# A transformer and state-space block on one core: three product groups with 512 moving columns are issued as halves of 256

## The chip, the cores and the metric

The kernel runs on one core of one Trainium2 chip. The metric is the device time of one execution in microseconds (us); three executions of the kernel before took 1441.66, 1443.39 and 1445.95 us, median 1443.39 us. The rows come from one profiled execution, with one clock for all engines of the core.

## The reference, cut to what matters

Two blocks are computed on 256 tokens of width 1024, all in fp32. The first ends in a layer of experts, the second in a feed-forward layer. Three sums of many products are what the change touches:

```python
# experts: 16384 experts, each with a row of u and a row of v; wgt is zero for those not chosen
wgt = gc * gelu(u . x)
out = einsum('chk,chkd->cd', wgt, vv)          # the kernel: W[256 x 16384] @ v[16384 x 1024]
# second block
h  = layer_norm(ALPHA * h + mix @ w_o)         # [256 x 1024] @ [1024 x 1024]
ff = square(relu(h @ w_up + b_up)) @ w_down    # the last: [256 x 4096] @ [4096 x 1024]
```

The kernel does not gather expert rows: it computes all 16384 activations, multiplies them by a gate matrix that is zero where an expert was not chosen, and multiplies the result by the whole of v.

## The kernel before, in words

**Products in three parts.** An fp32 matrix is split into a high part hi, rounded to the type fp32r, and a rest lo = x - hi. A product of x and w is then three matmuls, hi·hi, hi·lo and lo·hi, all accumulated in one place of PSUM. That is `mm3` (L219 to L225): L221 takes the high weights and the high moving operand, L224 the high weights and the low moving operand, L225 the low weights and the high moving operand. TensorE loads the weights anew ahead of every one of these matmuls. The first matmul of a sum carries `start=True`.

**The split.** `split_tile` (L193) takes a loaded tile `raw` of 128 x 1024, makes `hi` on ScalarE (L198) and `lo` on VectorE (L201). `raw`, `hi` and `lo` have three buffers each, so the split of a later tile waits until TensorE has finished with the tile three before. The loads are issued on SyncE's queue in a written order (L188).

**The order of the stages in the experts.** `expert_in` (L996) runs 128 times over tiles of u: the tile is the weights, the 256 tokens are the moving operand, and the output `ea` has 256 columns; 24 matmuls each. While it runs, `gates` (L1013) puts in groups of eight small fp16 matmuls of 128 columns (`gt`, L1034 and L1035). Then `sum_rows` (L1069) runs over 128 tiles of v ("terms"): `expert_out` (L1050) splits the 128 x 256 weights of that term into `whi` (L1056) and `wlo` (L1057), and the tile of v is now the moving operand. `rows_of` (L1060) goes over two halves h of the 1024 output columns for one group t of 128 tokens. The four sums `acc[t][h]` of 128 x 512 fp32 fill one PSUM bank each, named `pe` in the rows. One term is 2 x 2 x 3 = 12 matmuls with 512 moving columns.

**The last terms.** `sum_rows` holds back the last three terms and then goes bank by bank through `HALVES`: the three terms of bank (0,0), then of (0,1), (1,0), (1,1), each bank's first matmul ordered after the last of the bank before (`before`), so that VectorE can read a finished bank while TensorE fills the next.

**The same function twice more.** `w_o` (L1233) is `sum_rows` over 8 terms, `ff` (L1268) over 32 terms; in the latter each term is preceded by the 24 matmuls `up` (L1252, 256 moving columns) of a later feature tile, whose output becomes the weights of its own term. In all `rows_of` issues (128 + 8 + 32) x 12 = 2016 matmuls.

**Who orders the work.** The order of instructions on each engine is made when the program is built, by a scheduler that goes by the written order, by what is ready in its own simulated time, and by the written ordering edges (`after`). In `pe` it puts the four L221 of a term first and then four pairs of L224 and L225; in `ff` it keeps the written order L221, L224, L225. The other products of the second block, `pj` (L1424, 256 or 272 moving columns), have the moving operand hT, whose eight slices are 288 columns apart.

Of the kernel before, what the change touches and what calls it, by code (L numbers as in the profile page):

```python
# [81 lines left out]
class K:  # L82
# [977 lines left out]
    def rows_of(self, acc, t, x, v, first, last, before=None, halves=(0, 1)):  # L1060
        x = [z[:, t * 128:t * 128 + 128] for z in x]
        for h in halves:
            done = self.mm3(
                acc[t][h], x, [z[:, h * 512:h * 512 + 512] for z in v], first, last, before
            )
        self.last = done
        return done

# [788 lines left out]
```

## Time and profile before

| what | value |
|---|---|
| median of three executions | 1443.39 us |
| the profiled execution, its own time | 1441.46 us |
| its span, first to last instruction | 1439.7 us |
| TensorE busy | 1376.3 us, 96% |
| VectorE busy | 1126.6 us, 78% |
| ScalarE busy | 763.2 us, 53% |
| granted TensorE clock, mean | 0.985 |
| stage `ea` (first to last start) | 203.0 to 593.8 us |
| stage `pe` | 593.8 to 955.4 us |
| stage `w_o` | 1219.0 to 1242.2 us |
| stage `up` and `ff` | 1251.1 to 1427.7 us |

Matmuls overlap in TensorE's pipeline, so the duration of one is longer than the distance to the next; the distance from start to start is the pace at which TensorE works. "PEld" is the weight load of TensorE, which runs beside the matmul before it.

### The profile page before, as it was taken

The page shows a single profiled execution, that of the slowest core. Times are in us where ns is not written, and L with a number is a line of the kernel's source. Part 1 is how long each engine was busy: PE and PEld are TensorE (multiplying, and loading weights), DVE is VectorE, ACT ScalarE, POOL GpSimd, SP SyncE. Part 2 cuts the span into 40 slices and gives each one's busy share as a digit, 9 for nine tenths or more (in the row PEclk, how much of TensorE's full clock was granted, in tenths as well). Part 3 has the DMA queues.
Part 4 walks back from the last instruction along what each step waited for, and adds up shares of the span by engine and source line. Part 5 has one row for each costly group of instructions (what it writes and reads, how often), then busy time and mean ns, then how long its engine had stood idle before and what let it go on. Part 6 is the DMA issues. An engine that isn't in the chain of part 4 may idle for free.

```text
span 1439.7 us, 24324 instructions
## 1 busy us (share of the span) xinstructions
PE 1376.3 (96%) x9217; PEld 1216.1 (84%) x9217; DVE 1126.6 (78%) x2329; ACT 763.2 (53%) x1324; POOL 150.2 (10%) x128
## 2 busy tenths in 40 slices
PE   6897999999999999999999999998999999999996
PEld 3686999999999999988887788877876899889995
DVE  6888899977889897655566798668798978665556
ACT  3365555545555544544446468645474564455552
POOL 0133000000000000000000000014656600000001
PEclk9998999999999999999999999999999999999998
DMA  9774445554444445555557765534232455366552
GB/s 384 291 268 146 176 148 192 189 192 170 161 168 162 170 162 170 192 190 189 189 191 275 256 213 191 190 136 147 88 129 78 147 179 198 111 204 199 189 191 93
DMA packets 72287, 263.20 MB, mean 183 GB/s; under 512 B 8149, under 2 KB 8533, under 8 KB 71786
## 3 DMA queue, kind: packets, MB, share of 16 engines
q1 hardware_dynamic: 72170, 261.66, 52.5%
q8 instruction: 72, 1.18, 0.3%
q14 instruction: 45, 0.37, 0.1%
HBM read 259.53 MB, written 2.10 MB: 182 GB/s over the span
## 4 chain that ended last, share of the span: by engine, by line
PE 75%; DVE 15%; ACT 4%; DMA 2%; issue 2%; POOL 1%; DVEq 0%; ACTq 0%; POOLq 0%
PE pe L224 8%; PE pe L221 8%; PE pe L225 8%; PE ea L225 7%; PE ea L224 7%; PE ea L221 7%; DVE lo L201 4%; PE ff L224 2%; PE ff L221 2%; PE ff L225 2%; PE up L224 2%; PE up L225 2%; PE up L221 2%; PE pj L221 1%; PE pj L224 1%
## 5 line engine op out<-in xcount | busy, mean ns | idle before, releaser
L201 DVE TENSOR_TENSOR lo<-raw,hi 128x1024 fp32r<-128x1024 f32 x398 | 489.6, 1231 | 173.0 <-ACT hi L198 170.4
L198 ACT ACTIVATE hi<-raw 128x1024 fp32r<-128x1024 f32 x398 | 419.8, 1055 | 382.1 <-issue 87.9
L225 PE MATMUL ea<-h,lo 128*128 128x256 f32 x1024 | 285.6, 280 | 1.7 <-DVE lo L201 1.5
L221 PE MATMUL ea<-h,hi 128*128 128x256 f32 x1024 | 285.1, 279 | 0.8 <-ACT s_lo L1006 0.8
L224 PE MATMUL ea<-h,hi 128*128 128x256 f32 x1024 | 285.6, 279 | 0.0
L224 PE MATMUL pe<-lo,whi 128*128 128x512 f32 x512 | 200.1, 393 | 0.8 <-DVE lo L201 0.8
L225 PE MATMUL pe<-hi,wlo 128*128 128x512 f32 x512 | 198.7, 393 | 0.0
L225 PEld LDWEIGHTS ea<-h,lo 128*128 128x128 f32 x1024 | 192.1, 188 | 2.7 <-DVE lo L201 2.7
L221 PEld LDWEIGHTS ea<-h,hi 128*128 128x128 f32 x1024 | 192.5, 188 | 1.0 <-ACT s_lo L1006 1.0
L224 PEld LDWEIGHTS ea<-h,hi 128*128 128x128 f32 x1024 | 192.5, 188 | 0.0
L221 PE MATMUL pe<-hi,whi 128*128 128x512 f32 x512 | 143.5, 395 | 1.1 <-ACT hi L198 1.1
L224 PEld LDWEIGHTS pe<-lo,whi 128*128 128x128 f32 x512 | 96.1, 188 | 24.1 <-DVE lo L201 1.9
L221 PEld LDWEIGHTS pe<-hi,whi 128*128 128x128 f32 x512 | 95.6, 188 | 23.3 <-ACT hi L198 1.7
L225 PEld LDWEIGHTS pe<-hi,wlo 128*128 128x128 f32 x512 | 96.1, 188 | 21.9
L221 PE MATMUL pj<-hT,hi 128*128 128x256 f32 (+1 forms) x328 | 96.6, 294 | 0.0
L224 PE MATMUL pj<-hT,hi 128*128 128x256 f32 (+1 forms) x328 | 93.9, 286 | 2.5 <-DVE hT L217 2.5
L225 PE MATMUL pj<-hT,lo 128*128 128x256 f32 (+1 forms) x328 | 93.5, 286 | 0.0
L1056 ACT ACTIVATE whi<-s_lo 128x256 fp32r<-128x256 f32 x64 | 26.3, 417 | 78.2 <-PE pe L224 78.2
L221 PEld LDWEIGHTS pj<-hT,hi 128*128 128x128 f32 x328 | 62.8, 191 | 5.7 <-issue 2.7
L225 PE MATMUL up<-h1T,lo 128*128 128x256 f32 x240 | 66.9, 279 | 0.4 <-DVE lo L201 0.4
L221 PE MATMUL up<-h1T,hi 128*128 128x256 f32 x240 | 66.8, 279 | 0.2 <-ACT hi L198 0.2
L224 PE MATMUL up<-h1T,hi 128*128 128x256 f32 x240 | 67.0, 279 | 0.1
(471 smaller groups left out, 2745.4 us busy)
## 6 DMA issues: line engine op xcount, KB each, us to landing
raw<-in_u SPq DMA_DIRECT2D x128, 512.0 KB, 3.5
raw<-in_v SPq DMA_DIRECT2D x128, 512.0 KB, 4.2
raw<-in_sC SPq DMA_DIRECT2D x41, 512.0 KB, 3.5
raw<-in_down SPq DMA_DIRECT2D x32, 512.0 KB, 4.2
raw<-in_up SPq DMA_DIRECT2D x30, 512.0 KB, 4.2
s_hi<-in_ada SPq DMA_DIRECT2D x28, 512.0 KB, 6.0
raw<-in_sA SPq DMA_DIRECT2D x17, 512.0 KB, 4.3
s_hi<-in_sA SPq DMA_DIRECT2D x14, 512.0 KB, 6.2
```

The costliest lines, as they stand in the source:

```text
L198: self.last_hi = nc.scalar.activation(out=hi[:, 0:n], in_=raw[:, 0:n], func=AF.Copy)
L201: x = nc.vector.tensor_tensor(out=lo[:, 0:n], in0=raw[:, 0:n], in1=hi.bitcast(F32)[:, 0:n], op=ALU.subtract)
L221: i = mm(out, lhsT=w[0], rhs=x[0], start=first, stop=False)
L224: mm(out, lhsT=w[0], rhs=x[1], start=False, stop=False)
L225: return mm(out, lhsT=w[1], rhs=x[0], start=False, stop=last)
L1056: nc.scalar.activation(out=whi, in_=w, func=AF.Copy)
```

## The change

Each 512-column product of `rows_of` becomes two of 256 columns in the same bank: first the three parts for columns 0 to 255, then the three parts for columns 256 to 511. Only the first matmul of a sum's first half carries `start=True`; the ordering edge `before` goes to the first half alone. 2016 matmuls of 512 columns become 4032 of 256, with 4032 weight loads in place of 2016; the columns multiplied stay the same.

```diff
     def rows_of(self, acc, t, x, v, first, last, before=None, halves=(0, 1)):
         x = [z[:, t * 128:t * 128 + 128] for z in x]
         for h in halves:
-            done = self.mm3(
-                acc[t][h], x, [z[:, h * 512:h * 512 + 512] for z in v], first, last, before
-            )
+            for o in (0, 256):
+                done = self.mm3(
+                    acc[t][h][:, o:o + 256], x, [z[:, h * 512 + o:h * 512 + o + 256] for z in v],
+                    first and o == 0, last and o > 0, None if o else before,
+                )
         self.last = done
         return done
```

## Rows read from the trace of the kernel before

**Rows 1.** The page: span, busy time by engine, granted clock in 40 slices

```profile
span 1439.7 us, 24324 instructions
...
PE 1376.3 (96%) x9217; PEld 1216.1 (84%) x9217; DVE 1126.6 (78%) x2329; ACT 763.2 (53%) x1324; POOL 150.2 (10%) x128
...
PEclk9998999999999999999999999999999999999998
```

**Rows 2.** The page: the chain that ended last, by engine

```profile
PE 75%; DVE 15%; ACT 4%; DMA 2%; issue 2%; POOL 1%; DVEq 0%; ACTq 0%; POOLq 0%
```

**Rows 3.** Groups by line and shape: busy us, mean ns of one, idle before

```profile
L224 PE MATMUL pe<-lo,whi 128*128 128x512 f32 x512 | 200.1, 393 | 0.8 <-DVE lo L201 0.8
L225 PE MATMUL pe<-hi,wlo 128*128 128x512 f32 x512 | 198.7, 393 | 0.0
L221 PE MATMUL pe<-hi,whi 128*128 128x512 f32 x512 | 143.5, 395 | 1.1 <-ACT hi L198 1.1
...
L224 PE MATMUL ff<-lo,whi 128*128 128x512 f32 x128 | 50.4, 394 | 0.8 <-DVE lo L201 0.8
```

**Rows 4.** Busy time by stretch: length, busy us of each engine (instructions), clock, DMA

```profile
600.00:740.00 140.00, 140.00 (x608) 113.83 (x607) 83.45 (x102) 69.28 (x101) 0.00 (x0) 1.00 0.56 190
...
1260.00:1415.00 155.00, 154.55 (x1004) 140.02 (x1003) 91.69 (x119) 82.76 (x115) 0.00 (x0) 1.00 0.59 195
```

**Rows 5.** Timeline of TensorE in ea before the gates: start us, us

```profile
249.75 0.28 PE L221 MATMUL ea<-h,hi 128*128 128x256 f32 x1
...
255.98 0.28 PE L224 MATMUL ea<-h,hi 128*128 128x256 f32 x1
```

**Rows 6.** Timeline of TensorE in ea, behind a group of small gate matmuls

```profile
450.10 0.22 PE L1035 MATMUL gt<-oh_c,oh_a 128*128 128x128 f16 x1
...
450.43 0.22 PE L1035 MATMUL gt<-oh_c,oh_a 128*128 128x128 f16 x1
...
451.02 0.28 PE L221 MATMUL ea<-h,hi 128*128 128x256 f32 x1
...
453.61 0.28 PE L224 MATMUL ea<-h,hi 128*128 128x256 f32 x1
```

**Rows 7.** Timeline of TensorE in pj, 256 moving columns

```profile
1155.22 0.28 PE L225 MATMUL pj<-hT,lo 128*128 128x256 f32 x1
...
1157.88 0.28 PE L224 MATMUL pj<-hT,hi 128*128 128x256 f32 x1
```

**Rows 8.** Timeline of TensorE in the feed-forward stage: 24 up, 12 ff, next up

```profile
1290.93 0.28 PE L221 MATMUL up<-h1T,hi 128*128 128x256 f32 x1
...
1293.78 0.39 PE L221 MATMUL ff<-hi,whi 128*128 128x512 f32 x1
...
1296.54 0.28 PE L221 MATMUL up<-h1T,hi 128*128 128x256 f32 x1
```

**Rows 9.** Waits of ScalarE from 600 to 740 us: total us, times, longest

```profile
ACT whi L1056 <- PE pe L224: 69.6, 50, 1.5
```

**Rows 10.** Timeline of all engines at the end of pe: wait in brackets

```profile
940.92 1.06 ACT L198 ACTIVATE hi<-raw 128x1024 fp32r<-128x1024 f32 x1 [1.65 <-PE pe L225]
...
942.01 1.23 DVE L201 TENSOR_TENSOR lo<-raw,hi 128x1024 fp32r<-128x1024 f32 x1 [1.48 <-ACT hi L198]
...
948.84 0.50 PE L224 MATMUL pe<-lo,whi 128*128 128x512 f32 x1 [0.77 <-DVE lo L201]
```

**Rows 11.** Waits of TensorE, whole span: total us, times, longest us

```profile
PE pe L221 <- ACT hi L198: 1.1, 1, 1.1
...
PE ff L224 <- DVE lo L201: 0.8, 1, 0.8
PE pe L224 <- DVE lo L201: 0.8, 1, 0.8
PE w_o L224 <- DVE lo L201: 0.8, 1, 0.8
```

**Rows 12.** The page: the DMA queue that feeds instructions; packets, MB, share

```profile
q8 instruction: 72, 1.18, 0.3%
```

## The prediction

> **What bounds the kernel now.** I read the busy times first. TensorE is busy 96% of the span, and its granted clock is under nine tenths only in the fourth and the last of 40 slices [rows 1]; in the stretches used below it is 1.00, the level of 2.4 GHz [rows 4]. The chain that ended last lies on TensorE for 75% of the span [rows 2], so this engine sets the time. Busy time does not tell how fast it works, though: one 512-column matmul lasts 393 ns [rows 3], but the next starts much sooner. So I counted starts. From 600 to 740 us only `pe` matmuls run, 608 of them [rows 4]; two of these began before the stretch, so 606 starts in 140 us are one every 231.0 ns. In the same stretch TensorE never idles, while VectorE is busy for 83 of 140 us, ScalarE for 69 [rows 4], and ScalarE even stands waiting 69.6 us in all for TensorE to come to a certain matmul [rows 9]. `pe` is bound by TensorE's pace alone. In the feed-forward stretch it is the same: 154.55 us busy of 155 [rows 4]. The question is thus only: do two 256-column matmuls take more or less than 231.0 ns?
>
> **The change part by part.**
>
> *The pace of the halves.* 2016 products are split: 1536 in `pe`, 384 in `ff`, 96 in `w_o`. All lie on the path, since TensorE is the bound there. The trace has 256-column matmuls of the same type, each with its own weight load, at three paces. (a) In `ea`, before the gates come, 55 steps take 255.98 - 249.75 = 6.23 us, or 113.3 ns each [rows 5]. A pair is 226.6 ns: 4.4 ns less than now. (b) In `ea` behind a group of gate matmuls, 22 steps take 453.61 - 451.02 = 2.59 us, or 117.7 ns [rows 6]. A pair is 235.4 ns: 4.4 ns more. In the feed-forward stage, behind 512-column matmuls, 24 `up` take 1293.78 - 1290.93 = 2.85 us, 118.8 ns each, against 230.0 ns for each of the 12 `ff` that follow [rows 8]; that pair is 7.6 ns more than its neighbour. (c) In `pj` 23 steps take 1157.88 - 1155.22 = 2.66 us, or 115.7 ns [rows 7]. A pair is 231.3 ns: 0.3 ns more. So the pace of 256 columns is not one number: the same code runs at 113 or at 118, and `pj` lies between.
>
> I take `pj`, because it is nearest in where its operands lie. The moving operand of `ea` is a fixed tile whose slices are 256 columns apart, so every matmul starts at a like place. In `pj` the start moves by 288 columns from slice to slice. In `pe` the moving operand will go back and forth between the tiles `hi` and `lo`, whose buffers are 1056 columns each (`W`, L78), so the starts shift too. And 231.0 = 2 x 115.5 is what 512 columns give now with these very tiles. Cost: 2016 x 0.3 ns = +0.6 us. Ends for the range: 2016 x -4.4 = -8.9 us by (a), 2016 x 4.4 = +8.9 us by (b), and 2016 x 7.6 = +15.3 us by the worst block.
>
> The Trainium skill, page "TensorE: Matmul & The Clock Gate", section "Wait — 56ns, not 53.3ns?", gives every matmul a fixed cost of about 2.5 ns beside its columns at the full clock; by it the 2016 extra starts would cost an estimated 5.0 us. No row here shows that cost by itself: pace (a) lies under half of a 512-column step, which a fixed cost forbids, and pace (b) lies above it.
>
> *The weight loads.* 2016 more. At pace (a) there is one load to every 113.3 ns already, and small gate matmuls start six steps in 450.43 - 450.10 = 0.33 us, one pair of load and matmul every 55 ns [rows 6]. The load and its issue are covered by the matmul before at either width; I add nothing beyond the paces above, in which they are contained. If that cover failed, it would show as one of the slower paces.
>
> *Instructions to fetch.* The queue that feeds instructions moved 1.18 MB in all [rows 12]. If all of it were TensorE's 9217 loads and 9217 matmuls, 4032 more would be 0.26 MB, small beside 190 GB/s over 360 us [rows 4]. `ea` issues at the rate that `pe` will have and shows no stall. Zero.
>
> *The split of v, its buffers and the loads.* No load, ScalarE or VectorE instruction changes. A buffer of `hi` comes free with the last matmul of its term, as before, at the same time if the pace is the same. At 940.92 ScalarE had waited 1.65 us for this, and VectorE follows it at 942.01 [rows 10]; the tile then made is used two terms later, since there are three buffers. If TensorE became 9 us faster over 168 terms, a term would be 0.05 us shorter, and the 1.65 us of waiting covers it. Zero.
>
> *Order.* The scheduler sets the 24 matmuls of a term anew. Should it no longer put the high parts first, the first use of `lo` comes up to 4 x 231 = 924 ns sooner in a term. The cover is the lead of two terms, about 2 x 12 x 231 ns = 5.5 us, less the split itself, 1.06 + 1.23 us [rows 10]; so nothing shows.
>
> *The held terms.* In each of the three sums TensorE waits once for the last `lo`, 0.8 us, and in `pe` once for `hi`, 1.1 us [rows 11]. The second half of a bank isn't tied by `before`, so some of its matmuls may be put into the 0.8 us [rows 10]. Gain at most 3 x 0.8 = 2.4 us, if each hole is filled; loss at most the same, if the finish of a bank is delayed by such matmuls and the wait stays. I take 0: it is not written in the code which will happen, and what is late next, VectorE's reading of the last bank, needs all of them.
>
> *Sum.* 0.6 + 0 + 0 + 0 = +0.6 us on the profiled execution's 1441.46 us (its span 1439.7 and 1.8 around it), 0.04%. That execution lies 1.9 us under the median of the three; carried over to the median it is 1443.39 + 0.6 = 1444.0 us.
>
> **The rivals.**
>
> *Fast pace.* A stream of nothing but 256-column matmuls settles at (a), and `pe` would be such a stream, with no gates in it. For it: over the 6 us of rows 5 there is no slower step, and nothing in `pe` disturbs. Against: the moving operand's place shifts. It gives 1443.39 - 8.9 = 1434.5 us. The 720 matmuls of `up` would no longer stand behind 512-column ones either: at most 720 x (118.8 - 113.3) = 4.0 us more, so 1430.5 at the lowest.
>
> *Slow pace (the other side).* The place is the change-over from `hi` to `lo` as moving operand; if each change costs what follows a disturbance in `ea`, the pace is (b) throughout. It decides as soon as the pace is above 116.6 ns, since (2 x 116.6 - 231.0) x 2016 = 4.4 us. For it: 8 or 16 changes of tile in each term, and the neighbours of `ff` [rows 8]. Against: `pj`, with its shifting starts, and the fact that 512 columns do no worse than 231. Time: 1443.39 + 8.9 = 1452.3 us; with the `up` block's pace 1458.7.
>
> *A fixed cost at every start.* Then the half costs half plus something, the same in every state. Rows bound it by 2 x pace - 231.0: 0.3 by (c), 4.4 by (b); the middle, 2.35 ns, gives 2016 x 2.35 = 4.7 us, 1448.1 us. Pace (a) speaks against it. This is the form of the rule quoted from the Trainium skill above; by that page's own figure the time would be an estimated 1448.4 us.
>
> *The order goes wrong.* If the lead on `lo` were lost, TensorE would wait up to 0.9 us in each of 128 terms, over 100 us. The ScalarE waits speak against it [rows 9]. That the change doesn't do what it says, the compiler joining the halves again, would show as 9217 matmuls once more, at the old time; TensorE now loads weights before every matmul [rows 1], even where they repeat, so nothing is joined today.
>
> **How the numbers follow.** About 0.3%, 4.3 us, is what a measurement of this kernel can tell from no change. Unchanged pace 0.42 (with 0.01 for joined halves), fast pace 0.25, slow pace 0.23, fixed cost 0.07, wrong order 0.03. The first lies within 0.3%: its own range is 1440 to 1448 us, from the 2.4 us of the holes and about a nanosecond of pace either way. Fast pace is faster by 0.6%, the other three slower: 0.25, 0.42, 0.33. Both signs together hold most of the chance, so the range must take in both paces: 1433 to 1454 us. It leaves out the lower end of the fast case, the upper end of the slow one and the wrong order, somewhat under 2 in 10.
>
> **What would show it.** In the changed profile: 11233 matmuls and as many weight loads; `pe` rows of 128x256, x1024 each, with a duration near the 0.28 us of `ea` [rows 5] in place of 393 ns; start-to-start steps in `pe` near 115.5 ns (113 or 118 for the two rivals); the stage `pe` as long as before to 2 us, `ff` likewise; the waits of TensorE for `lo` 0 to 0.8 us in each sum. A `pe` stage 7 us shorter means the fast pace, 7 us longer the slow one. If the stages keep their length and the total still moves, the reasoning on pace was beside the point and the order of other work was what counted.

## The result and the profile after

The changed kernel takes 1455.2 us (median of 10 executions, 1448.61 to 1458.09) against 1445.13 us for the kernel before on the same chip (10 executions). The ratio is 1.0062, with a 95% interval of 1.0044 to 1.0081: slower, on the side of the rival "slow pace" and 1.2 us beyond the upper end of the range. The profiled execution took 1449.4 us, 7.9 more than that of the kernel before.

The page of the changed kernel: span, busy time, granted clock, the queue that feeds instructions, the chain that ended last, and the groups that answer to [rows 3].

```profile
span 1447.6 us, 28552 instructions
...
PE 1380.3 (95%) x11329; PEld 1316.1 (91%) x11329; DVE 1128.7 (78%) x2329; ACT 762.4 (53%) x1324; POOL 148.0 (10%) x128
...
PEclk9997999999999999999999999999999999999999
...
q8 instruction: 88, 1.44, 0.4%
...
PE 75%; DVE 15%; ACT 3%; DMA 3%; issue 2%; POOL 2%; DVEq 0%; ACTq 0%; POOLq 0%
...
L224 PE MATMUL pe<-lo,whi 128*128 128x256 f32 x1024 | 285.4, 280 | 2.5 <-DVE lo L201 2.5
...
L225 PE MATMUL pe<-hi,wlo 128*128 128x256 f32 x1024 | 283.1, 279 | 0.0
L221 PE MATMUL pe<-hi,whi 128*128 128x256 f32 x1024 | 282.4, 280 | 0.5 <-ACT hi L198 0.5
...
L224 PE MATMUL ff<-lo,whi 128*128 128x256 f32 x256 | 72.1, 282 | 0.9 <-DVE lo L201 0.9
```

Nothing but TensorE's list has changed: the same count of instructions on VectorE and ScalarE, the clock as high as before, and 75% of the chain on TensorE as in [rows 2]. But there are 11329 - 9217 = 2112 more matmuls, not 2016: `sum_rows` also serves the output projection of the first block, called `wo` below, with two sums of 4 terms and 12 products to a term. That is 96 products more than the 2016 counted before. Next, the same two stretches as in [rows 4].

```profile
600.00:740.00 140.00, 140.00 (x1199) 140.00 (x1198) 83.79 (x107) 69.00 (x102) 0.00 (x0) 1.00 0.61 187
1260.00:1415.00 155.00, 154.93 (x1323) 154.73 (x1323) 93.52 (x128) 80.44 (x115) 0.00 (x0) 1.00 0.61 194
```

Two of the 1199 matmuls began before 600 us, so there is a start every 140 / 1197 = 117.0 ns, a pair every 234.0 instead of 231.0, at the same granted clock of 1.00. TensorE still never idles. The pace has become worse, and the stage longer: the view of the tile `pe` gives the first and the last start of each of its lines.

```profile
L221 PE MATMUL pe<-hi,whi x1024: 276/279/388, 597.6 to 964.6; 128*128 128x256 f32 x171
...
L225 PE MATMUL pe<-hi,wlo x1024: 275/279/288, 598.6 to 964.8; 128*128 128x256 f32 x171
```

964.8 - 597.6 = 367.2 us, against 955.4 - 593.8 = 361.6 before. The same view for `ea`, `w_o`, `up` and `ff`:

```profile
L221 PE MATMUL ea<-h,hi x1024: 276/276/366, 208.1 to 597.3; 128*128 128x256 f32 x171
```

```profile
L221 PE MATMUL w_o<-hi,mix x64: 276/281/288, 1225.0 to 1248.4; 128*128 128x256 f32 x64
...
L225 PE MATMUL w_o<-hi,mix x64: 275/280/286, 1225.3 to 1248.6; 128*128 128x256 f32 x64
```

```profile
L221 PE MATMUL up<-h1T,hi x240: 276/276/383, 1257.4 to 1422.8; 128*128 128x256 f32 x120
```

```profile
L225 PE MATMUL ff<-hi,wlo x256: 277/281/288, 1266.9 to 1435.5; 128*128 128x256 f32 x128
```

`w_o` now takes 23.6 us (23.2 before), `up` with `ff` 178.1 us (176.6 before). So these three stages together are 5.6 + 0.4 + 1.5 = 7.5 us longer, of the 7.9 us between the two profiled executions. The rest moved too, but nearly cancels: `ea` starts 5.1 us later, it is 1.3 us shorter, and so is the stretch from `pe` to `w_o`, by 3.4 us. The medians are 10.1 us apart; what the further 2 us are, no trace shows.

The waits of TensorE in the whole span, and of ScalarE from 600 to 740 us (total, times, longest), answer to [rows 11] and [rows 9]:

```profile
PE wo L224 <- DVE lo L201: 5.2, 1, 5.2
...
PE pe L224 <- DVE lo L201: 2.5, 4, 0.9
...
PE w_o L224 <- DVE lo L201: 0.9, 1, 0.9
PE ff L224 <- DVE lo L201: 0.9, 1, 0.9
PE pe L221 <- ACT hi L198: 0.5, 1, 0.5
```

```profile
ACT whi L1056 <- PE pe L224: 70.0, 49, 1.6
```

The waits in `pe` grew by 1.1 us (2.5 + 0.5 against 0.8 + 1.1). ScalarE still waits 70 us for TensorE, so nothing upstream is late. The 5.2 us in `wo` were 1.5 before, a matter for an experiment. The timeline of TensorE shows what the pace is made of (start, length); here are the ends of three terms in a row.

```profile
682.50 0.28 PE L225 MATMUL pe<-hi,wlo 128*128 128x256 f32 x1
...
684.54 0.28 PE L225 MATMUL pe<-hi,wlo 128*128 128x256 f32 x1
684.65 0.28 PE L221 MATMUL pe<-hi,whi 128*128 128x256 f32 x1
...
687.36 0.28 PE L225 MATMUL pe<-hi,wlo 128*128 128x256 f32 x1
687.48 0.28 PE L221 MATMUL pe<-hi,whi 128*128 128x256 f32 x1
...
690.11 0.28 PE L224 MATMUL pe<-lo,whi 128*128 128x256 f32 x1
```

18 steps in 2.04 us are 113.3 ns each; the next 23 in 2.71 us are 117.8; the next 22 in 2.63 us are 119.5. One stream, one clock, no wait, and three paces that change with the term. What differs between terms is the buffers. One buffer of `hi` or `lo` is 1056 columns, 4224 bytes, which is 16.5 times 256: neighbouring buffers start 128 bytes apart modulo 256. By the addresses in the built program, `hi` and `lo` both start at 0 in the first of these terms, both at 128 in the second, and at 0 and 128 in the third; the high and low weights of the three start at 64 and 192, both at 64, and at 64 and 192. (Below, "at 64" means an SBUF start address of 64 modulo 256 bytes.)

In the feed-forward stage, the block of 24 `up` and the 24 `ff` behind it:

```profile
1296.86 0.28 PE L221 MATMUL up<-h1T,hi 128*128 128x256 f32 x1
...
1299.71 0.28 PE L221 MATMUL ff<-hi,whi 128*128 128x256 f32 x1
...
1302.54 0.29 PE L221 MATMUL up<-h1T,hi 128*128 128x256 f32 x1
```

`up` takes 2.85 us, 118.8 ns a step, as in [rows 8]; the 24 `ff` take 2.83 us, 117.9 ns a step, so a pair takes 235.8 ns where one product took 230.0.

### The profile page after: what moved, and what is told of

The parts are those of the page before. It is cut to its first block, busy times and chain, and to the rows that moved or that the text cites. A ratio compares the mean times of both kernels' runs of the same rounds, so it can differ in the third digit from the quotient of the medians.

```text
span 1447.6 us, 28552 instructions
## 1 busy us (share of the span) xinstructions
PE 1380.3 (95%) x11329; PEld 1316.1 (91%) x11329; DVE 1128.7 (78%) x2329; ACT 762.4 (53%) x1324; POOL 148.0 (10%) x128
## 3 DMA queue, kind: packets, MB, share of 16 engines
q8 instruction: 88, 1.44, 0.4%
## 4 chain that ended last, share of the span: by engine, by line
PE 75%; DVE 15%; ACT 3%; DMA 3%; issue 2%; POOL 2%; DVEq 0%; ACTq 0%; POOLq 0%
PE ea L225 8%; PE pe L224 7%; PE pe L221 7%; PE ea L224 7%; PE pe L225 7%; PE ea L221 7%; DVE lo L201 4%; PE ff L224 2%; PE ff L225 2%; PE ff L221 2%; PE up L224 2%; PE up L225 2%; PE up L221 2%; PE pj L221 1%; PE pj L224 1%
## 5 line engine op out<-in xcount | busy, mean ns | idle before, releaser
L224 PE MATMUL pe<-lo,whi 128*128 128x256 f32 x1024 | 285.4, 280 | 2.5 <-DVE lo L201 2.5
L225 PE MATMUL ea<-h,lo 128*128 128x256 f32 x1024 | 285.6, 280 | 1.2 <-DVE lo L201 1.0
L224 PE MATMUL ea<-h,hi 128*128 128x256 f32 x1024 | 285.7, 279 | 0.0
L221 PE MATMUL ea<-h,hi 128*128 128x256 f32 x1024 | 285.1, 279 | 0.0
L225 PE MATMUL pe<-hi,wlo 128*128 128x256 f32 x1024 | 283.1, 279 | 0.0
L221 PE MATMUL pe<-hi,whi 128*128 128x256 f32 x1024 | 282.4, 280 | 0.5 <-ACT hi L198 0.5
L224 PEld LDWEIGHTS pe<-lo,whi 128*128 128x128 f32 x1024 | 192.4, 188 | 3.3 <-DVE lo L201 3.3
L225 PEld LDWEIGHTS ea<-h,lo 128*128 128x128 f32 x1024 | 192.1, 188 | 2.2 <-DVE lo L201 2.2
L224 PEld LDWEIGHTS ea<-h,hi 128*128 128x128 f32 x1024 | 192.5, 188 | 0.0
L221 PEld LDWEIGHTS ea<-h,hi 128*128 128x128 f32 x1024 | 192.5, 188 | 0.0
L225 PEld LDWEIGHTS pe<-hi,wlo 128*128 128x128 f32 x1024 | 191.9, 188 | 0.0
L221 PEld LDWEIGHTS pe<-hi,whi 128*128 128x128 f32 x1024 | 190.8, 188 | 0.8 <-ACT hi L198 0.7
L221 PE MATMUL pj<-hT,hi 128*128 128x256 f32 (+1 forms) x328 | 96.6, 295 | 0.0
L224 PE MATMUL pj<-hT,hi 128*128 128x256 f32 (+1 forms) x328 | 93.9, 286 | 2.5 <-DVE hT L217 2.5
L225 PE MATMUL pj<-hT,lo 128*128 128x256 f32 (+1 forms) x328 | 93.7, 286 | 0.0
L224 PE MATMUL ff<-lo,whi 128*128 128x256 f32 x256 | 72.1, 282 | 0.9 <-DVE lo L201 0.9
L225 PE MATMUL ff<-hi,wlo 128*128 128x256 f32 x256 | 71.4, 281 | 0.0
L221 PE MATMUL ff<-hi,whi 128*128 128x256 f32 x256 | 71.3, 281 | 0.0
L221 PEld LDWEIGHTS pj<-hT,hi 128*128 128x128 f32 x328 | 63.0, 192 | 5.3 <-issue 3.5
```

Source lines behind the costliest of these rows:

```text
L221: i = mm(out, lhsT=w[0], rhs=x[0], start=first, stop=False)
L224: mm(out, lhsT=w[0], rhs=x[1], start=False, stop=False)
L225: return mm(out, lhsT=w[1], rhs=x[0], start=False, stop=last)
```

## The experiments

Means of steps below are over all start-to-start distances of neighbouring matmuls of one tile and width, those of twice the median or more left out as waits; sums keep the waits. In the kernel before, a 512-column step of `pe` has a mean of 232.0 ns; in the changed kernel, a step of 256 has 117.3.

My theory, "place": where the operands start in SBUF, modulo 256 bytes, sets the pace of 256-column streams, and `hi` and `lo` lie badly to each other. Rivals: "start", every matmul start costs something fixed; "order", the scheduler's new order costs, most of all in the `wo` stage with its 5.2 us.

**e1: hi and lo in one buffer.** With 2 x 1056 columns to a buffer and `lo` 1024 columns behind `hi`, all moving starts of `pe`, `ff` and `w_o` are at 0.

```diff
-        hi = self.st.tile([128, W], F32R, tag="hi", name="hi", bufs=3)[:, o:o + 1024]
-        lo = self.st.tile([128, W], F32R, tag="lo", name="lo", bufs=3)[:, o:o + 1024]
+        both = self.st.tile([128, 2 * W], F32R, tag="hi", name="hilo", bufs=3)
+        hi, lo = both[:, o:o + 1024], both[:, 1024 + o:1024 + o + 1024]
```

> The changed kernel, with hi and lo of a split tile in one buffer whose size is a multiple of 256 bytes, lo 4096 bytes behind hi: every moving slice of pe, ff, w_o then starts at the same place modulo 256 bytes. Theory 'place' (halves run at the slow pace because the starts of successive moving slices differ modulo 256 bytes): steps in pe fall from 117.3 to about 113.5 ns, in ff from 118.6 to about 114.5, so 3072 x 3.8 + 768 x 4 = 15 us less than the changed kernel: 1440 us, ratio to before 0.997. Theory 'start' (every matmul start costs a fixed 2 to 3 ns, wherever the operands lie): steps stay at 117, 1455 us, ratio 1.006.

**e2: the same, lo 128 bytes further.** Each engine gets e1's instructions in e1's order; only the place of `lo` differs.

```diff
-        hi, lo = both[:, o:o + 1024], both[:, 1024 + o:1024 + o + 1024]
+        hi, lo = both[:, o:o + 1024], both[:, 1056 + o:1056 + o + 1024]
```

> As e1_same_place, with the same order of instructions on every engine, but lo lies 128 bytes further: hi and lo differ by 128 modulo 256 bytes in every term. Theory 'place': pe steps near 119.5 ns in every term, as now in the third of the terms whose tiles lie so: 3072 x (119.5 - 113.5) = 18 us more than e1_same_place, 1460 us, ratio 1.01. Theory 'start': equal to e1_same_place within 2 us, steps equal.

e1: 1456.23 us, ratio 1.0066 (1.0045 to 1.0087). e2: 1462.61 us, 1.0119 (1.0081 to 1.0156). Timeline of TensorE in `pe`, first e1, then e2:

```profile
699.75 0.28 PE L225 MATMUL pe<-hilo,wlo 128*128 128x256 f32 x1
...
703.04 0.28 PE L224 MATMUL pe<-hilo,whi 128*128 128x256 f32 x1
```

```profile
699.80 0.28 PE L221 MATMUL pe<-hilo,whi 128*128 128x256 f32 x1
...
703.02 0.28 PE L221 MATMUL pe<-hilo,whi 128*128 128x256 f32 x1
```

In e1 29 steps take 3.29 us, 113.4 ns; in e2 27 take 3.22 us, 119.3 ns. Over the stage the steps sum to 357.1 and 369.9 us: 12.8 us from 128 bytes. A fixed cost at each start can't do that, nor can order: both are the same in the two. Yet in total they are only 6.4 us apart, where 18 were expected, and e1 as a whole is no faster than the change, where 15 us less were expected. The reason stands in stages that were not touched: there `hi` and `lo` are the weights, and now start alike. The tile `ym`, e1 first, then e2:

```profile
L221 PE MATMUL ym<-yin,hilo x64: 277/281/281, 1209.9 to 1232.2; 128*128 128x256 f32 x64
...
L225 PE MATMUL ym<-yin,hilo x64: 280/281/282, 1210.2 to 1232.4; 128*128 128x256 f32 x64
```

```profile
L221 PE MATMUL ym<-yin,hilo x64: 276/276/279, 1219.9 to 1241.3; 128*128 128x256 f32 x64
...
L225 PE MATMUL ym<-yin,hilo x64: 276/276/281, 1220.1 to 1241.6; 128*128 128x256 f32 x64
```

191 steps take 22.5 us in e1, 117.8 ns each, and 21.7 us in e2, 113.6. Likewise `ea` sums to 359.8 us in e1 and 356.2 in e2, against 352.8 in the changed kernel.

**e3: e1's buffer, 512 columns.** The edit of e1 in the kernel before.

> The kernel before (512 columns) with the buffers of e1_same_place. Theory 'place', if it holds for 512 columns too: steps in pe fall from 231.0 to about 227, 1632 x 4 = 6.5 us and some in ff, 1437 us, ratio 0.994. If only halves can settle at the fast pace: 231, ratio 1.000. Theory 'start': ratio 1.000 as well.

1454.92 us, ratio 1.0062 (1.0042 to 1.0082). The 512-column steps have a mean of 232.9 ns: starting alike gains them nothing. The joint buffer thus costs some 9 us, most of it outside `pe`, which explains why e1 is no faster than the change. But e1 isn't faster than e3 either, 1.3 us above it: its `pe` runs from first to last start in 360.9 us against 363.4, and its `ea`, in which the two kernels have the same instructions, in 396.6 against 394.6. Why `ea` differs was not found; in total the pair is inconclusive.

**e4 and e5: wo alone, and all but wo.** In e4 only the two `wo` sums (4 terms each) are halved, in e5 only the others (`n != 4`).

```diff
+            n = 256 if self.halved else 512
+            for o in range(0, 512, n):
...
+        self.halved = n == 4
```

> Only the sums of the first block's output projection (wo, 96 products) are split; pe, w_o and ff keep 512 columns. Theory 'order' (in the changed kernel the new order of that stage makes TensorE wait 5.2 us for a lo and the next stage starts 3.4 us later): pq starts 3 to 4 us later than before, total 1448.5, ratio 1.0025. If pace alone cost anything there: 192 halves x 2.5 ns = 0.5 us, ratio 1.0003.

> pe, w_o and ff are split, wo keeps 512 columns: the counterpart of e4_wo_only. Theory 'place': all of the loss is in the pace of pe, ff and w_o: pe 6.4 us longer than before, ff and w_o 2 us, total 1453.5 us, ratio 1.0055. Rival 'wo order': the 3.4 us by which the stage of wo grew in the changed kernel's trace are part of the loss, so without them 1450.5 to 1451 us, ratio 1.0035.

e4: 1443.64 us, ratio 0.9989 (0.997 to 1.0009). e5: 1453.3 us, 1.0056 (1.0035 to 1.0076). The halves of `wo` alone cost nothing that can be measured, and without them the loss is nearly all there, so it is in `pe`, `ff` and `w_o`. The wait of 5.2 us itself is not tested by e4, whose waits in `wo` are others:

```profile
PE wo L225 <- DVE mg L217: 2.8, 1, 2.8
...
PE wo L224 <- DVE lo L201: 1.6, 1, 1.6
```

What is left for "order" in that stage is the gap between e5 (8.1 us above its kernel before) and the change (10.1 us), and their intervals do not tell these two apart.

**e6 to e8: a layout for both kinds of operand.** Buffers of 1088 columns (17 times 256 bytes), `lo`'s 128 bytes off `hi`'s, and `lo` of a moving tile written 32 columns further: moving starts alike, weights 128 bytes apart. A constant tile is cut to make room. e6 has the halves, e7 has 512 columns, e8 has the halves but in `wo`.

```diff
-W = 1024 + 32
+W = 1024 + 64
...
+        if self.gapped is None:
+            self.place(self.st, 32)
+            self.gapped = True
+        p = o + 32 if moving else o
-        lo = self.st.tile([128, W], F32R, tag="lo", name="lo", bufs=3)[:, o:o + 1024]
+        lo = self.st.tile([128, W], F32R, tag="lo", name="lo", bufs=3)[:, p:p + 1024]
```

> The changed kernel with hi and lo in buffers of their own, as before, but of 1088 columns (4352 bytes, 17 times 256), the lo buffers 128 bytes off, and the lo of a moving tile written 32 columns further: moving slices of pe, wo, w_o and ff all start at the same place modulo 256 bytes, weight slices of hi and lo in ea, up, ym stay 128 apart as in most of the kernel before. The order of instructions is that of the changed kernel. Theory 'place': pe steps 113.5 ns (117.3 in the changed kernel), ff about 115, ea and ym as before: 3072 x 3.8 + 768 x 3.5 = 14 us less than the changed kernel, 1441 us, ratio 0.997. Theory 'start': 1455 us, ratio 1.006.

> The kernel before with the buffers of e6_layout_split. In e3_before_same 512 columns did not settle at a fast pace though all starts were alike (232.9 ns a step), so: pe steps 231 to 233, total 1445 us, ratio 1.000 +- 0.002. If the 512 columns settle after all: 227, 1438 us, ratio 0.995.

> e5_not_wo with the buffers of e6_layout_split. Theory 'place': pe steps 113.5, total 1438 to 1441 us, ratio 0.995 to 0.997, better than both kernels; if the wo order counts, it is the lower of the two numbers and 3 us below e6_layout_split. Theory 'start': equal to e5_not_wo.

e6: 1447.86 us, ratio 1.0019 (0.9999 to 1.004). e7: 1452.58, 1.0045 (1.0025 to 1.0066). e8: 1448.05, 1.002 (1.0004 to 1.0036). Here halving is a gain of 4.7 us (e6 against e7), though their intervals overlap. But all three are some 7 us slower than expected, for the layout itself loses: e7 stands 7.4 us above the kernel before. A part of that is in `ea`: the layout moved the tile that `ea` reads from 192 to 64, and `ea`'s steps now sum to 355.5 us with a median of 117 ns, where before they had 353.2 and 114.

**e9 to e12: that tile put back.** One gap is 32 columns wider, so `ea`'s moving slices are at 192 again. e9 has the halves; e10 has them with `lo` unshifted, thus 128 bytes off `hi`; e11 leaves `wo` at 512; e12 has 512 throughout.

```diff
-        self.place(self.rr, 16)
+        self.place(self.rr, 48)
```

> The layout of e6_layout_split with one edit: the gap ahead of the ring from which ea's moving slices come is 32 columns wider, so that those slices start at 192 instead of 64 in units of bytes modulo 256, as they do in the kernel before (where ea's 3072 steps sum to 353.2 us) and in e2 (median 113 ns). pe, ff and w_o stay at 256 columns with all moving slices alike modulo 256. Theory 'place': pe stays near a sum of 355 to 359 us and 113 ns in the median, and ea comes down from e6's 355.5 to 351 to 354 us, so 1443 to 1446 us. Rival 'the rest of the layout': what this layout costs (1452.6 us for it with 512 columns) has nothing to do with ea's place; then ea stays at 355 and the time at 1448.

> e9_layout2_split with one edit: lo of the moving tiles is written where the buffer begins, so that hi and lo are 128 bytes apart modulo 256 in pe, ff and w_o; the order of instructions on every engine is the same. Theory 'place': pe's 3072 steps go from a median of 113 to 118 ns, their sum from some 357 to 367 to 370 us, ff's mean from 116 to 118.6 ns: 12 to 15 us longer than e9. Rival 'order of the work': the time is that of e9 within 3 us.

> e9_layout2_split with the 96 products of wo in the first stage kept at 512 columns. Theory 'place': as e9 within 2 us, for wo is 2 times 96 steps of some 3 ns. It would be over 3 us faster than e9 if the order of the work in the wo stage cost what its one longer wait suggests.

> The layout of e9_layout2_split with 512 columns everywhere, as in the kernel before. Theory 'place': the products of 512 columns take 231 to 233 ns at any place, so pe's 1536 steps sum to 356 to 358 us, and this stands 2 to 6 us above e9, as e7 stood 4.7 us above e6. Theory 'start', that each start costs 2.5 ns by itself: it stands 5 us below e9.

e9: **1439.67 us, ratio 0.9955 (0.9938 to 0.9973)**, faster than both kernels, though TensorE's list of instructions is that of the changed kernel, in the same order. e10: 1454.2 us, 1.0061 (1.0038 to 1.0085). e11: 1441.19, 0.9964 (0.9948 to 0.9981). e12: 1442.64, 0.9981 (0.9963 to 0.9999). The `pe` matmuls of TensorE from 600 to 740 us (length, busy us, matmuls, clock, DMA share, GB/s), for e9, e10 and e12:

```profile
600.00:740.00 140.00, 140.00 (x1238) 1.00 0.65 193
```

```profile
600.00:740.00 140.00, 140.00 (x1187) 1.00 0.63 186
```

```profile
600.00:740.00 140.00, 140.00 (x607) 1.00 0.58 190
```

With two begun earlier taken off, that is 113.3, 118.1 and 231.4 ns a step. The pair e9 and e10, same instructions in the same order, is 14.5 us apart, and "place" said 12 to 15. `ea` came down to 350.8 us, as expected. That is 4.7 us of the 8.2 by which e9 is under e6 (on another chip); e9 came out lower than the 1443 to 1446 us expected, and the rest was not traced. e12 lies 3.0 us above e9, within the 2 to 6 expected and against "start", which wanted e12 below. So of the 6.7 us by which e9 beats the kernel before, 3.0 are the halves and 3.7 the layout; the intervals of e9 and e12 just overlap. e11 is within 2 us of e9. A part of the faster pace is given back, though: e9's waits in `pe`, whole span,

```profile
PE pe L226 <- ACT hi L203: 3.0, 2, 2.3
PE pe L229 <- DVE lo L206: 2.8, 4, 0.9
```

are 5.8 us against 1.9 in [rows 11] (L226 and L229 are L221 and L224 in the kernel before).

**e13 to e16: which property of the place?** Open was whether alike is enough, or the place itself counts, or the place against that of the weights, which in `pe` start at 64 and 192 in this layout. In e9, with both moving parts at 0, they are put elsewhere; e16 sets `hi` at 0 and `lo` at 64. The edit for e13, where both are at 128 (in e14 the two numbers are 16 and 48, in e15 48 and 16, in e16 0 and 48):

```diff
-        hi = self.st.tile([128, W], F32R, tag="hi", name="hi", bufs=3)[:, o:o + 1024]
+        q, p = (o + 32, o + 0) if moving else (o, o)
+        hi = self.st.tile([128, W], F32R, tag="hi", name="hi", bufs=3)[:, q:q + 1024]
```

> e9_layout2_split with hi and lo of the moving tiles both written 128 bytes further: all moving starts of pe, ff and w_o at 128 modulo 256 bytes instead of 0; the order of instructions is the same. Theory 'alike' (what counts is that successive moving operands start alike): pe's median stays 113 ns and its sum 355 to 359 us, the time within 3 us of e9. Theory 'absolute place' (a start at 0 or 192 is fast, one at 64 or 128 slow): pe at 117 to 118 ns, sum 365 to 368 us, 10 to 13 us above e9. In the changed kernel the terms with both at 128 ran at 117.8, so I think the second the likelier.

> As e13, with all moving starts of pe, ff and w_o at 64 modulo 256 bytes; the high and low weights start at 64 and 192. Theory 'alike': 113 ns, within 3 us of e9. Theory 'absolute place', read from ea in e6 (moving at 64, median 117): 117 to 118 ns, 10 us above e9 or more.

> As e13, with all moving starts of pe, ff and w_o at 192 modulo 256 bytes. Both theories expect the fast pace, 113 ns and within 3 us of e9. If it is slow, what counts is the place of the moving operand against that of the weights (64 and 192 here; in ea 0 and 128), and not the place itself.

> As e9, with hi of the moving tiles at 0 and lo at 64 modulo 256 bytes, so that successive starts differ by 64 instead of 128 bytes as in e10. Theory 'alike': slow, 117 to 119 ns, as e10. Theory 'absolute place' (64 is slow): a third of the steps has a slow start, so between e9 and e10, 114 to 117 ns.

e13: 1441.8 us, ratio 0.9975 (0.9954 to 0.9996). e14: 1456.73, 1.0079 (1.0053 to 1.0104). e15: 1458.77, 1.0086 (1.0056 to 1.0116). e16: 1455.26, 1.007 (1.0045 to 1.0094). The same row of each, in this order:

```profile
600.00:740.00 140.00, 140.00 (x1238) 1.00 0.64 194
```

```profile
600.00:740.00 140.00, 140.00 (x1180) 1.00 0.61 185
```

```profile
600.00:740.00 140.00, 140.00 (x1178) 1.00 0.60 184
```

```profile
600.00:740.00 140.00, 140.00 (x1184) 1.00 0.62 187
```

Worked out as above: 113.3, 118.8, 119.0 and 118.4 ns. Both of my readings fail. Alike is not enough: at 64 and at 192 the moving parts start alike and are slow. The absolute place is not it either: 128 is fast, against what I thought likelier, and 192, fast in `ea`, is slow here, the outcome that e15's text gave to the place against the weights. What fits these four, e9 and e10 is that two things are needed: successive moving operands alike modulo 256, and 64 bytes off the weights modulo 128.

| run | moving hi, lo at | weights at | pe, mean step |
|---|---|---|---|
| e9 | 0, 0 | 64, 192 | 114.0 ns |
| e13 | 128, 128 | 64, 192 | 114.0 ns |
| e14 | 64, 64 | 64, 192 | 119.8 ns |
| e15 | 192, 192 | 64, 192 | 119.9 ns |
| e10 | 0, 128 | 64, 192 | 118.7 ns |
| e16 | 0, 64 | 64, 192 | 118.7 ns |

This rule is a fit, not shown beyond these six. `ym` in e1 points to a third thing: it is slow with its moving operand at 192, as in e2, and all weights at 0, while in e2 its high and low weights are 128 bytes apart. The traces, taken term by term, say the same (a term counts as fast when its median step is 113 or 114 ns; the places are from the built programs). In the changed kernel no term with `hi` and `lo` 128 bytes apart is fast: 42 of the 128 terms in `pe`, all 32 in `ff`. Of the 45 `pe` terms with `hi` and `lo` alike and the weights 128 bytes apart, 36 are fast; of the 41 with the weights alike as well, 4. In `ff` of e6, where all moving starts are alike, 16 of 16 terms with the weights apart are fast and none of 16 with the weights alike. Yet in `pe` of e9, whose moving starts never change, 47 of the 50 terms with alike weights are fast: alike weights seem to keep a slow stream slow more than they slow a fast one. This is read from traces; no run moves the weights of `pe` alone.

Nor does place settle the pace by itself. `ea` in e6 has moving starts at 64 against weights at 0 and 128, and a median of 117 ns; `ym` in the same run, with the same starts modulo 256, has 113. And `glu`, a stage of 256-column matmuls that the edits don't touch, has the same instructions in the same order at the same addresses in e9 and e13. Its first and last starts, e9 first, then e13:

```profile
L226 PE MATMUL glu<-yg,hi x64: 276/276/384, 1180.0 to 1201.6; 128*128 128x256 f32 x64
...
L230 PE MATMUL glu<-yg,lo x64: 276/276/283, 1180.4 to 1201.8; 128*128 128x256 f32 x64
```

```profile
L226 PE MATMUL glu<-yg,hi x64: 278/280/392, 1174.4 to 1197.0; 128*128 128x256 f32 x64
...
L230 PE MATMUL glu<-yg,lo x64: 278/279/284, 1174.7 to 1197.2; 128*128 128x256 f32 x64
```

That is 21.8 against 22.8 us, a median of 113 against 118 ns, at a granted clock of 1.00 in both. So a stream also seems to keep the pace into which it has fallen. What the hardware does with these addresses stays open.

## Why the prediction was wrong

*What bounds the kernel* was right: TensorE's pace alone. The clock, the chain and ScalarE's wait (70.0 us against [rows 9]) are as they were.

*The pace of the halves* is the step that failed: "I take `pj`, because it is nearest in where its operands lie", with a pair 0.3 ns above the 512-column step. Measured over whole stages, a pair is dearer by 2 x 117.28 - 231.97 = 2.6 ns in `pe`, by 2 x 118.56 - 231.12 = 6.0 in `ff` and by 2 x 118.07 - 232.39 = 3.7 in `w_o`. With 1536, 384 and 96 products that is 4.0 + 2.3 + 0.4 = 6.7 us, where the prediction has 0.6; it carries most of the profiled 7.9 us. The ground for choosing the row was sound, for place does decide; but the row was 23 steps out of a stage: over all of `pj` the 256-column steps of the kernel before have a median of 117 ns, not 115.7. With it the sum would have been 2016 x (2 x 117 - 231) = 6.0 us, or 1449.4 us, slower. With their mean, 119.2, it would have been 14.9 us; so the whole row would have given the sign, and its size only within these two.

*The weight loads, the instructions, the split and its buffers* at zero: right as far as shown. 4224 more loads and matmuls took 0.26 MB more on the instruction queue (1.44 against [rows 12]), just the figure worked out for 4032, and e9 runs at 113.3 ns with the loads in place. When TensorE does become faster, though, the waits in `pe` rise to 5.8 us (e9), 4.2 of them between 755 and 860 us and 1.6 at the end: the 1.65 us of ScalarE's slack did not cover them.

*Order*: the scheduler did drop the four leading L221 (the timeline runs L225, L221, L224 in turn), and apart from the held terms nothing showed, as said. *The held terms* at 0 cost 1.1 us in `pe`, within the 2.4 allowed. *Counting*: the 96 products of `wo` were missed; e4 shows no cost of them. What the 5.2 us wait in that stage is worth stays open within the 2 us between e5 and the change.

*The rivals.* "Slow pace" happened, at 117 to 118.6 ns, over the 116.6 from which it was to decide; its mechanism, the change of tile from `hi` to `lo`, slows a stream when the two start apart (e10 and e16), and in the changed kernel that holds for all terms of `ff` and for 42 of the 88 slow ones in `pe`. The other 46 have `hi` and `lo` alike, and in 37 of them the high and low weights start alike too. The place against the weights (e14, e15) has no part in this loss, for the moving starts are at 0 and 128 there and the weights at 64 and 192 throughout. "Fast pace" was as real: with better places it is e9, where the halves gain 3.0 us against e12 and 8.9 were worked out. In `pe` the steps without the waits gain 6.3 us there (354.1 to 347.8 us), but with the waits only 3.1 (360.3 to 357.2). "Fixed cost" falls by e9, e12 and e13. The Trainium skill, page "TensorE: Matmul & The Clock Gate", section "Wait — 56ns, not 53.3ns?", gives a fixed cost of about 2.5 ns to each matmul. No fp32r stream here agrees: the fastest tenth of the 512-column steps before takes 226 ns or less, and the 256-column steps of e9 take 113.3, one half, with no room for a cost that does not halve. For 128 columns that section of the Trainium skill has 55 to 56 ns measured. The fp16 gate matmuls of [rows 6], at 55 ns a step, agree with that.

*The range.* It stood on 1443.39 us, the median of three executions, where ten gave 1445.13; that shift alone is more than the 1.2 us by which 1455.2 lies outside. What failed is the size of one term: +0.6 us in all was forecast and +10.1 measured.

## What to carry to other kernels

Where a stream of short matmuls is the bound and runs at two paces that no wait and no clock explains, look at the start addresses of its operands: move one operand by 64 or 128 bytes, keep everything else, and compare whole stages, for the same code at the same places can run at either pace (`glu` in e9 and e13). The split itself was worth -3.0 and -4.7 us in two layouts with better places (e9 against e12, e6 against e7), +1.3 us in a third (e1 against e3), and +10.1 us with the places that the buffers happened to have; the first two are little more than the spread of the runs could hide, and the third is within it. And take the pace of a nearest row from its whole stage, not from a window of some twenty steps.

## What was not expected of the hardware

128 bytes in the place of one moving operand changed the pace of a 256-column fp32r stream from 113.3 to 118.1 ns a step at the same granted clock (e9, e10); 64 bytes in both did the same (e14). The weights' places count too: `ym` went from 113.6 to 117.8 ns when its high and low weights started alike (e2, e1). Streams of 512 columns showed nothing of this, with means of 232.0, 232.9, 232.4 and 232.3 ns in the kernel before, e3, e7 and e12, though they too have steps of 226 ns. And one stage took 21.8 or 22.8 us with the same instructions at the same addresses (`glu` in e9, e13).
